# Source order on the compute engines, and mixer visits pipelined by hand, in a hybrid mLSTM/GLA encoder layer

## The chip, the cores and the metric

The kernel runs on one core of a Trainium2 chip. A core has five engines, each with an instruction stream of its own: TensorE (matrix products, PE in the profile; its weight loads are PEld), VectorE (DVE), ScalarE (ACT), GpSimd (POOL) and SyncE (SP, which here only issues DMAs). They wait for one another by semaphores. The metric is the device time of one execution in microseconds; lower is better.

## The reference

One encoder layer on a sequence of 1024 tokens with 1024 features, in float32: a token mixer, then a gated MLP, each between RMSNorms and added to the residual.

```python
def hybrid_mixer(hn, w_in, ...):
    proj = jnp.matmul(hn, w_in)
    a_qk, a_v, a_o, a_gates, b_q, b_k, b_v, b_r, b_lr = jnp.split(proj, idx, axis=-1)
    qk = silu(dwconv3(a_qk, mlstm_conv_w, mlstm_conv_b))          # q and k of 4 mLSTM heads
    i_fw, f_fw, i_bw, f_bw = jnp.split(a_gates + mlstm_gate_b, 4, axis=-1)
    h = mlstm_chunkwise(...forward...) + flip(mlstm_chunkwise(...backward...))
    y_a = sigmoid(a_o) * head_rms_norm(h, mlstm_norm)
    la = log_sigmoid(lr @ w2 + gb) / 16                           # decay per key dimension, both directions
    o = gla_chunkwise(...forward...) + flip(gla_chunkwise(...backward...))
    y_b = silu(b_r) * head_rms_norm(o, gla_norm)                  # 4 GLA heads
    return jnp.matmul(concatenate([y_a, y_b]), w_out)

x = x + rms_norm(hybrid_mixer(rms_norm(x), ...))
x = x + rms_norm(conv_ffn(rms_norm(x), ...))
```

Both scans go in both directions. Within a chunk they are products of queries and keys weighted by decays; between chunks a state is carried by "decay times state plus keys times values".

## The kernel before, in words

The sequence is cut into 8 chunks of 128 tokens. The kernel normalises and transposes the input, and computes a first strip of the projection that holds the gate columns and half of the GLA values (product `vacc`, up to about 48 us). Then two generators run interleaved:

- `proj()` computes the rest of the projection in 11 groups of 256 columns. Each matrix is split in a high and a low half, so one output takes three products. `f_block` makes 128 columns by 512 tokens (`facc`, 24 products 512 wide), `t_block` 256 tokens by 256 columns (`tacc`, 48 products 256 wide). Both `yield` three times within a block, and once more after the block's result is taken out of PSUM, so a block is four steps; each group begins with an empty step. The order is GLA keys and queries (`in_bqk`), GLA values (`in_v`, which sets `bv`), the convolved mLSTM queries and keys (`in_aqk`, `aqk`: VectorE adds the neighbours in lines 454 and 455, and after two blocks multiplies by the tanh in line 466), mLSTM values (`av`), and two gate groups (`in_gate`, `gate`). Weights of the next group are loaded and split (`wprep`, `ahead`, line 113) at the end of a group's second block.
- `mix()` is everything that needs the projection: `gla_decay` (eight products `z`, ScalarE's Abs, Exp and Ln, then VectorE lines 390, 391 and 393), `gate_rows` (row-wise gate arithmetic with four scans, lines 316 to 360), their transposes (`ptc`), then `gla()`, `mlstm()` and `out_weights()`.

In `gla()`, `levels(c)` makes a chunk's weighted scores in eight levels (64, 32, 16, 8, 4, 2, 1, 0): GpSimd takes differences `D`, ScalarE their exponential `E`, VectorE multiplies it into queries and keys (`Q`, `K`, `kz`), TensorE makes the products `sc`, and they are kept in `Pt`. `states()` makes each chunk's state (`ptk`, `U`, then `state_step` in line 537), forward as the chunks come and backward in a loop after them. `finish(c)` makes a chunk's output `o` and its head norm. `mlstm()` has `states()` (`ptm`, `KT`, `Um`, `both_step`), and for each chunk `decays` (loads and exponentials `RB`, `RI`), `front` (`sr`) and `back` (`nd`, and the division). `out_weights()` loads eight slabs of the output weights through three buffers that later hold gated rows (`yv`, `gv`), and splits them (lines 108 and 109). `prep(t)` loads and gates the rows of the output projection and transposes them (`pt`, line 888); the output product is `oacc`.

What sets the order of the work: the program is traced by `_interleave`, which gives each generator's step a weight (a projection step 0.25, a mixer step 1.0 or what it yields). From that order a planner places the instructions of each engine by its own estimates of when their inputs are ready; it decides the final order in each engine's stream and in SyncE's queue of DMAs. On the chip each stream is then executed in that order.

PSUM, where products land, has eight banks: `pe` (2: `E`, `th`, half of the mLSTM products), `ps` (3: `z`, `ptc`, `sc`, `U`, `ptk`, `o`, `sr` and others) and `mm` (3: the projection's blocks). A tile takes a bank until its last reader is done.

After the projection come the output projection (from about 440 us), and the MLP, whose products (lines 1063 and 1221) fill the rest.

Of the kernel before, what the change touches and what calls it, by code (L numbers as in the profile page):

```python
# [17 lines left out]
P = 128  # L18
# [5 lines left out]
H = 4  # L24
# [12 lines left out]
W_PROJ = 0.25  # L37
R_AUX, R_COLS, R_GLA, R_STATES, R_ML, R_OUT = 3.4, 0.6, 0.7, 0.7, 1.9, 2.0
# [4 lines left out]
def _interleave(*gens):  # L43
    live = [[g, w, 0.0] for g, w in gens]
    while live:
        e = min(live, key=lambda v: v[2])
        e[2] += e[1]
        try:
            w = next(e[0])
            if w is not None:  # L50
                e[1] = w
        except StopIteration:
            live.remove(e)
# [3 lines left out]
def tile_encoder_layer(  # L57
# [84 lines left out]
    def wprep(src, segs):  # L142
        n = sum(s[1] for s in segs)
        wh = wp.tile([P, NK, 256], F32R, name="wh")
        wl = wp.tile([P, NK, 256], F32R, name="wl")
        for g in range(4):
            raw = wp.tile([P, 2, 256], F32, name="wraw", bufs=3)
            o = 0
            for c0, w in segs:
                nc.sync.dma_start(raw[:, :, o:o + w], src[:, 2 * g:2 * g + 2, c0:c0 + w])  # L150
                o += w
            split(wh[:, 2 * g:2 * g + 2, 0:n], wl[:, 2 * g:2 * g + 2, 0:n], raw[:, :, 0:n])
        return wh, wl
# [147 lines left out]

    def gate_rows():
# [13 lines left out]
        nc.vector.tensor_scalar(out=gi, in0=gi, scalar1=gb[:, 0:1], scalar2=None, op0=ALU.add)  # L316
# [12 lines left out]
        rm = rw.tile([R, NC, P], F32, name="rm")  # L329
        nc.gpsimd.memset(rb, 0.0)  # L330
# [38 lines left out]
        yield  # L369
        for c in range(NC):  # L370
# [4 lines left out]
            yield R_COLS * W_PROJ  # L375
        yield R_AUX * W_PROJ

# [30 lines left out]
    def ahead(b=1):  # L408
        c = next(groups, None) if b == 1 else None
        if c is not None:  # L410
            ready.append(wprep(w_in, ((c, 256),)))

    ahead()

    def in_bqk(c0, dst, scale):
        wh, wl = ready.pop(0)
# [10 lines left out]
    def in_v(c0, dst, gs=(0, 1)):  # L427
        for g in gs:
            wh, wl = ready.pop(0)
# [11 lines left out]
    def in_aqk():  # L441
        for g in range(2):
            wh, wl = ready.pop(0)
# [26 lines left out]
    def in_gate(c0, off, silu):  # L470
        for g in range(2):
            wh, wl = ready.pop(0)
            yield
            for q in range(4):
# [10 lines left out]
                if q % 2:  # L485
                    nc.sync.dma_start(dG[q // 2].rearrange("(t p) n -> p t n", p=P)[:, :, off + 256 * g:off + 256 * g + 256], s)
                yield
# [11 lines left out]
    def mix():  # L499
        yield R_AUX * W_PROJ  # L500
        yield from gla_decay()
        yield from gate_rows()
        rctx.close()
        while "bq" not in done:
            yield
        gp = mctx.enter_context(tc.tile_pool(name="gp", bufs=2, reuse_waits="tile"))
        mslots = gp.tile([P, NC, H, P + 1], F32, name="mslots", bufs=1)
# [4 lines left out]

        nc.gpsimd.memset(mslots[:, 0], 0.0)
# [25 lines left out]
        def head_norm(pool, o, dst, i, c):  # L539
# [4 lines left out]
            v = pool.tile([P, H], F32, name="rs_v")  # L544
            nc.vector.tensor_scalar(out=v, in0=ss, scalar1=1.0 / DV, scalar2=EPS, op0=ALU.mult, op1=ALU.add)
            nc.gpsimd.tensor_tensor(out=hr[:, c, i, :], in0=v, in1=mhalf[:, 0:H], op=ALU.pow)
            nc.sync.dma_start(dst, o.rearrange("p h e -> p (h e)"))

        def gla():
# [23 lines left out]
            def states():  # L573
                for c in range(NC):
                    S = lp.tile([P, H, P + 1], F32, name="S")
                    nc.sync.dma_start(S, dS[c // 4][c % 4])
                    kk = load(lp, "kk", dkk[c])
                    v = v_tile(lp, dvb, c)
                    nc.scalar.activation(gam[:, c, :], S[:, :, P], AF.Exp, scale=1.0 / TEMP)
                    E = edge_decay(S, hi, lo)  # L580
                    kd = w2k("Q", 3)
                    nc.vector.tensor_tensor(out=kd, in0=E, in1=kk, op=ALU.mult)
                    yield
                    pt = ps.tile([P, H, P], F32, name="ptk", tag="ps")
                    for h in range(H):
                        nc.tensor.transpose(pt[:, h, :], kd[:, h, :], ident)
                    KT = w2k("KT", 1)
                    nc.scalar.copy(out=KT, in_=pt)
                    yield
                    U = ps.tile([P, H, P], F32, name="U", tag="ps")  # L590
                    for h in range(H):
                        nc.tensor.matmul(U[:, h, :], KT[:, h, :], v[:, h, 0:P], start=True, stop=True)
                    state_out(slots, c, [(0, H, U)])
                    if 1 <= c < NC - 1:
                        state_step(slots, lambda c, h: gam[:, c, h:h + 1], c, 0)
                    yield
                for c in range(NC - 2, 0, -1):
                    state_step(slots, lambda c, h: gam[:, c, h:h + 1], c, 1)
                    yield

            def levels(c):
# [6 lines left out]
                kk = load(lp, "kk", dkk[c])  # L608
# [6 lines left out]
                def weigh(L):  # L615
# [9 lines left out]
                    Q, K = w2k("Q", 3), None  # L625
# [689 lines left out]
```

## Time and profile before

| | |
|---|---|
| Median of 3 runs | 1189.55 us (1189.26 to 1192.82) |
| The profiled execution | 1189.67 us, span 1187.9 us |
| TensorE busy | 1151.1 us, 97% of the span |
| VectorE, ScalarE, GpSimd busy | 878.7, 591.4, 166.5 us |
| Mean granted TensorE clock | 0.989 |
| Projection and mixer | from 48.4 us to about 440 us |

How to read the lines. A group line is: line of the kernel, engine, operation, output tile <- input tiles, shapes, count, then busy time, mean nanoseconds of one, and the idle time before them with what ended it. A line by stretches is: from:to in us, the length, then for PE, PEld, DVE, ACT and POOL the busy time and (x instructions), then the granted TensorE clock, the share of DMA time and GB/s. A waits line is: who waited, for whom, us in total, times, the longest. A line of the timeline or of the chain is: start, duration, what. In the timeline, neighbours of one kind are merged (x count), and since instructions overlap, the time of several together is less than the sum of their means. Matrix products are pipelined: the time of one says little, the distance from one to the next is what it costs.

### The profile page before, as it was taken

The numbers are of one execution on the slowest core, as the hardware profiler recorded it, in microseconds if no ns is written. First come the engines' busy times: TensorE is split into PE (matmuls) and PEld (weight loads), VectorE is DVE, ScalarE is ACT, GpSimd is POOL, SyncE is SP. The second block draws the span as 40 slices with busy tenths as digits, with TensorE's granted clock in tenths as the row PEclk, the third lists the DMA queues.
The fourth block names the chain that finished last, engine by engine and source line by source line (L and its number), as shares of the span: only waits on it lengthen the run. The fifth ranks groups of instructions, "written<-read, shape, count | busy, mean of one in ns | idle before, by whom it ended". The sixth has DMA issues, their size and how long they took to land.

```text
span 1187.9 us, 21230 instructions
## 1 busy us (share of the span) xinstructions
PE 1151.1 (97%) x7896; PEld 979.7 (82%) x7896; DVE 878.7 (74%) x1604; ACT 591.4 (50%) x1271; POOL 166.5 (14%) x240
## 2 busy tenths in 40 slices
PE   8999999999999969999999999999999999999997
PEld 7989778888989968878788888888888878888885
DVE  5676669777433557667998888888888877987666
ACT  6572686878556534446543243433433245445451
POOL 1200425665054200101000000000000000000001
PEclk9999999999989989999999999999999999999999
DMA  7453675554777385542144342333224238754245
GB/s 201 149 134 102 169 223 155 152 171 127 189 197 209 117 278 186 178 141 80 36 142 142 109 132 64 113 123 108 89 81 133 98 123 299 252 178 133 81 137 190
DMA packets 134651, 175.77 MB, mean 148 GB/s; under 512 B 24964, under 2 KB 89860, under 8 KB 134548
## 3 DMA queue, kind: packets, MB, share of 16 engines
q1 hardware_dynamic: 134116, 172.58, 47.3%
q0 software_dynamic: 432, 1.84, 0.4%
q8 instruction: 62, 1.02, 0.3%
q14 instruction: 41, 0.34, 0.1%
HBM read 126.78 MB, written 47.53 MB: 147 GB/s over the span
## 4 chain that ended last, share of the span: by engine, by line
PE 73%; DVE 7%; ACT 6%; DMA 6%; issue 3%; POOL 3%; SPq 1%; DVEq 0%; POOLq 0%; ACTq 0%
PE pr L1063 35%; PE pr L1221 17%; PE facc L171 5%; PE oacc L1002 4%; PE tacc L182 4%; PE vacc L262 2%; DMA qq<-dmqq 1%; DMA yv<-dya 1%; DMA oraw<-in_w_out_dram 1%; DVE kz L637 1%; ACT sq L543 1%; DVE slots L537 1%; POOL RB L786 1%; POOL D L621 1%; POOL D L622 1%
## 5 line engine op out<-in xcount | busy, mean ns | idle before, releaser
L1063 PE MATMUL pr<-T,ah 128*128 128x512 f32 x704 | 217.2, 389 | 1.3 <-DVE G L1101 1.3
L1063 PE MATMUL pr<-B,ah 128*128 128x512 f32 x528 | 162.8, 390 | 0.0
L1063 PEld LDWEIGHTS pr<-T,ah 128*128 128x128 f32 x704 | 132.1, 188 | 29.4 <-DVE G L1101 1.8
L1063 PE MATMUL pr<-T,al 128*128 128x512 f32 x352 | 137.0, 389 | 0.0
L182 PE MATMUL tacc<-wh,xh 128*128 128x256 f32 x448 | 130.5, 291 | 0.0
L182 PE MATMUL tacc<-wl,xh 128*128 128x256 f32 x448 | 130.0, 290 | 0.0
L182 PE MATMUL tacc<-wh,xl 128*128 128x256 f32 x448 | 127.1, 284 | 0.0
L1221 PE MATMUL pr<-dwl,dah 128*128 128x512 f32 x308 | 120.0, 390 | 0.7 <-DVE dwl L113 0.7
L1221 PE MATMUL pr<-dwh,dal 128*128 128x512 f32 x308 | 120.1, 390 | 0.0
L1221 PE MATMUL pr<-dwh,dah 128*128 128x512 f32 x308 | 119.3, 390 | 0.0
L1063 PEld LDWEIGHTS pr<-B,ah 128*128 128x128 f32 x528 | 99.0, 188 | 20.4
L1063 PE MATMUL pr<-B,al 128*128 128x512 f32 x264 | 102.7, 389 | 0.0
L112 ACT CAST dah<-ar 128x512 fp32r<-128x512 f32 x77 | 47.6, 621 | 98.0 <-PE pr L1221 44.2
L182 PEld LDWEIGHTS tacc<-wh,xh 128*128 128x128 f32 x448 | 85.5, 191 | 2.7 <-issue 0.2
L182 PEld LDWEIGHTS tacc<-wl,xh 128*128 128x128 f32 x448 | 85.5, 191 | 1.4
L182 PEld LDWEIGHTS tacc<-wh,xl 128*128 128x128 f32 x448 | 85.7, 191 | 0.3
L112 ACT CAST ah<-fraw 128x512 fp32r<-128x512 f32 x64 | 39.6, 619 | 82.7 <-PE pr L1063 49.7
L113 DVE TENSOR_TENSOR dal<-ar,dah 128x512 fp32r<-128x512 f32 x77 | 53.0, 690 | 37.0 <-ACT dah L112 36.7
L1063 PEld LDWEIGHTS pr<-T,al 128*128 128x128 f32 x352 | 66.1, 188 | 13.6
L112 ACT CAST ah<-sa 128x512 fp32r<-128x512 f32 x44 | 27.4, 622 | 83.6 <-DVE sa L943 52.9
L1221 PEld LDWEIGHTS pr<-dwl,dah 128*128 128x128 f32 x308 | 57.8, 188 | 13.1 <-DVE dwl L113 1.1
L1221 PEld LDWEIGHTS pr<-dwh,dal 128*128 128x128 f32 x308 | 57.8, 188 | 12.9 <-DVE dal L113 0.9
(292 smaller groups left out, 2536.0 us busy)
## 6 DMA issues: line engine op xcount, KB each, us to landing
ar<-dA SPq DMA_DIRECT2D x77, 256.0 KB
wraw<-in_w_in_dram SPq DMA_DIRECT2D x48, 256.0 KB
fraw<-in_ffn_w_gate_dram SPq DMA_DIRECT2D x22, 512.0 KB
fraw<-in_ffn_w_up_dram SPq DMA_DIRECT2D x22, 512.0 KB
dA<-s SPq DMA_DIRECT2D x20, 512.0 KB
dA<-sx SPq DMA_DIRECT2D x10, 768.0 KB
Y<-in_ffn_w_down_dram SPq DMA_DIRECT2D x22, 256.0 KB
S<-dS SPq DMA_DIRECT2D x16, 258.0 KB
```

What stands on the lines that cost most here:

```text
L112: nc.scalar.copy(out=hi, in_=src)
L113: nc.vector.tensor_tensor(out=lo, in0=src, in1=hi.bitcast(F32), op=ALU.subtract)
L171: nc.tensor.matmul(acc, w[:, k, cs], v[:, k, hs], start=(k == 0 and n == 0), stop=(k == NK - 1 and n == 2))
L182: nc.tensor.matmul(acc[:, i, :], v[:, k, ts], w[:, k, :], start=(k == 0 and n == 0), stop=(k == NK - 1 and n == 2))
L262: nc.tensor.matmul(acc, v[:, k, ts], w[:, k, :], start=(k == 0 and n == 0), stop=(k == NK - 1 and n == 2))
L537: nc.vector.scalar_tensor_tensor(out=sl[rs, o, h, :], in0=sl[rs, c, h, :], scalar=sc(c, h)[rs], in1=sl[rs, o, h, :], op0=ALU.mult, op1=ALU ...
L543: nc.scalar.activation(sq, o[:, h, :], AF.Square, accum_out=ss[:, h:h + 1])
L621: nc.gpsimd.tensor_tensor(out=dv[:, :, :, 0, :], in0=ref, in1=xv[:, :, :, 0, :], op=ALU.subtract)
L622: nc.gpsimd.tensor_tensor(out=dv[:, :, :, 1, :], in0=xv[:, :, :, 1, :], in1=ref, op=ALU.subtract)
L1002: nc.tensor.matmul(accs[hf], v[:, j, :], w[:, k, hf * 512:(hf + 1) * 512], start=(k == 0 and n == 0), stop=(k == NK - 1 and n == 2))
L1063: nc.tensor.matmul(acc, A[i][:, k, :], B[b][j][:, k, :], start=(k == 0 and n == 0), stop=(k == 3 and n == 2))
L1221: nc.tensor.matmul(accs[i], o[v][:, ts], o[w], start=(p == 0 and n == 0), stop=(p == NP - 1 and n == 2))
```

## The change

The change has three parts.

1. The interleaved part is placed in source order on TensorE, ScalarE, VectorE and GpSimd; SyncE's queue stays with the planner. `_interleave` now has a main generator (the mixer) and a filler (the projection): the mixer yields how many projection steps are to follow.
2. The mixer's work is cut into visits with `load`, `prep` and `emit`. In `gla()`, at visit k the loads of visit k+3, the preparation of visit k+2 and the products of visit k are emitted, then the projection steps. A visit is one pair of levels of a chunk, or one chunk's state. State products come a visit after their transposes. The backward state steps are dealt over the last state visit and chunk 1's first two visits. The mLSTM states, decays and fronts are shifted against each other likewise, and the output weights are loaded three slabs ahead.
3. Smaller moves: the copy of the backward half of `U` goes from ScalarE to VectorE; gate rows are interleaved with the decays, two decays apart; the split of a weight group is dealt over projection steps (`todo`); the head norm's last two operations come a visit later; the first keys and values of the mLSTM are loaded in tiles of their own; the first gated rows may start when half of the last gate group is out (`half`).

```diff
-W_PROJ = 0.25
-R_AUX, R_COLS, R_GLA, R_STATES, R_ML, R_OUT = 3.4, 0.6, 0.7, 0.7, 1.9, 2.0
+F_HEAD, F_DECAY, F_GATES, F_COLS = 8.0, 2.0, 8.0, 1.0
+F_LEAD, F_FIRST, F_STATES, F_GLA, F_TURN = 1.5, 2.0, 1.8, 1.9, 2.0
+F_MSTATES, F_ML, F_OUT = 1.2, 4.4, 2.0
...
+def _interleave(main, filler):
+    due = 0.0
+    for n in main:
+        due += n
+        while due >= 1.0:
+            next(filler, None)
+            due -= 1.0
+    for _ in filler:
+        pass
...
     def wprep(src, c0):
...
+        todo.append(lambda: [load(g) for g in range(3)])
+        todo.append(lambda: None)
+        todo.append(lambda: None)
         for g in range(4):
+            todo.append(lambda g=g: cut(g))     # split; after g == 0 also load(3)
...
     def mix():
-        yield from gla_decay()
-        yield from gate_rows()
+        gates_ = gate_rows()
+        next(gates_)
+        yield F_HEAD
+        for n, _ in enumerate(gla_decay()):
+            if n % 2:
+                next(gates_, None)
+            yield F_DECAY
+        for _ in gates_:
+            pass
+        yield F_GATES
+        yield from gate_cols()
...
         def state_out(sl, c, parts):
...
-                    nc.scalar.copy(out=sl[64:128, c - 1, h0:h0 + n, :], in_=u[64:128])
+                    nc.vector.tensor_copy(sl[64:128, c - 1, h0:h0 + n, :], u[64:128])
...
+                def emit_(j):                    # a state visit: U of chunk j-1, transposes of chunk j
...
+                    if j == NC:
+                        back_steps(0)
...
+            def back_steps(n):
+                for c in range(NC - 2 - 2 * n, NC - 4 - 2 * n, -1):
                     state_step(slots, lambda c, h: gam[:, c, h:h + 1], c, 1)
...
+                LV = ((64, 32), (16, 8), (4, 2), (1, 0))
+                def prep(n):
+                    pairs[n] = [(L, weigh(L)) for L in LV[n]]
...
+                def emit_(n):
+                    if c > 0 and n == 0:
+                        vo[c - 1] = v_tile(lp, dvb, c - 1)
+                    if c > 0 and n == (3 if c == 1 else 1):
+                        finish(c - 1)
+                    st["emit"](n)
+                    if c == 1 and n < 2:
+                        back_steps(n + 1)
...
+            vs = pair_visits(0) + state_visits()
+            for c in range(1, NC):
+                vs += pair_visits(c)
+            for k in range(-3, len(vs)):
+                if k + 3 < len(vs):
+                    vs[k + 3].load()
+                if k >= -2 and k + 2 < len(vs):
+                    vs[k + 2].prep()
+                if k < 0:
+                    yield F_LEAD
+                    continue
+                while vs[k].gate and vs[k].gate not in done:
+                    yield 1
+                vs[k].emit()
+                yield vs[k].fill
...
             for c in range(NC):                  # mlstm
                 if c + 2 < NC:
-                    decays(c + 2)
+                    decay_load(c + 2)
+                while late:
+                    late.pop()()
+                back(c)
                 if c + 1 < NC:
                     front(c + 1)
+                if c + 2 < NC:
+                    decays(c + 2)
+                yield F_ML
...
+    def filler():
+        for _ in proj():
+            if todo:
+                todo.pop(0)()
+            yield
+
+    E = mybir.EngineType
+    with tc.manual_schedule(engines={E.PE, E.Activation, E.DVE, E.Pool}):
+        _interleave(mix(), filler())
```

More of the change, by code (lines that the diff above doesn't have):

```diff
@@ L35, with __init__ @@
 BIG = 1e30
-W_PROJ = 0.25
-R_AUX, R_COLS, R_GLA, R_STATES, R_ML, R_OUT = 3.4, 0.6, 0.7, 0.7, 1.9, 2.0
+F_HEAD, F_DECAY, F_GATES, F_COLS = 8.0, 2.0, 8.0, 1.0
+F_LEAD, F_FIRST, F_STATES, F_GLA, F_TURN = 1.5, 2.0, 1.8, 1.9, 2.0
+F_MSTATES, F_ML, F_OUT = 1.2, 4.4, 2.0
 C_AQK, C_AV, C_AO, C_AG = 0, 512, 1024, 1536
 C_BQ, C_BK, C_BV, C_BR, C_LR = 1552, 1808, 2064, 2576, 3088
[L43 to L53, printed above, removed]
+def _interleave(main, filler):
[7 more added lines that the diff above has]
+        pass
+class Visit:
+    def __init__(self, fill, emit, prep=None, load=None, gate=None):
+        self.fill, self.emit, self.gate = fill, emit, gate
+        self.prep, self.load = (f or (lambda: None) for f in (prep, load))
 @with_exitstack
@@ L329, in gate_rows @@
         rm = rw.tile([R, NC, P], F32, name="rm")
+        rows["gate"] = (gi, gf, rm)
         nc.gpsimd.memset(rb, 0.0)
@@ L368, in gate_rows, with gate_cols @@
         yield
-        yield
+    def gate_cols():
+        gi, gf, rm = rows["gate"]
         for c in range(NC):
@@ L428, in in_v @@
         for g in gs:
-            wh, wl = ready.pop(0)
+            wh, wl = group()
             yield
@@ L590, in states @@
[L590 to L597, printed above, removed]
+                    nc.scalar.activation(gam[:, j, :], S[:, :, P], AF.Exp, scale=1.0 / TEMP)
@@ new lines, in emit, with pair_visits, load_ @@
+                def emit(n):
+                    products(pairs.pop(n))
+                    if n == 3:
+                        for b in range(4):
+                            bs = slice(32 * b, 32 * b + 32)
+                            nc.scalar.copy(out=Pt[bs, :, bs], in_=acc[bs])
+                return prep, emit
+            def pair_visits(c):
+                st = {}
+                def load_():
+                    st["prep"], st["emit"] = chunk(c)
+                def emit_(n):
[6 more added lines that the diff above has]
+                        back_steps(n + 1)
+                return [Visit(F_GLA if c else F_FIRST, lambda n=n: emit_(n), lambda n=n: st["prep"](n), load_ if n == 0 else None)
+                        for n in range(4)]
@@ L859, in out_weights, with load @@
         gpost = ow["gpost"] = op.tile([P, D], F32, name="gpost")
-        for k in range(NK):
-            raw = op.tile([P, D], F32, name="oraw", tag=("yv", "yv", "gv")[k % 3], bufs=(2, 2, 1)[k % 3])
-            nc.sync.dma_start(raw, w_out[:, k, :])
-            split_scaled(woh[:, k, :], wol[:, k, :], raw, hg[:, k, :])
-            yield
+        raws = {}
+        def load(k):
+            raws[k] = op.tile([P, D], F32, name="oraw", tag=("yv", "yv", "gv")[k % 3], bufs=(2, 2, 1)[k % 3])
+            nc.sync.dma_start(raws[k], w_out[:, k, :])
+        for k in range(3):
+            load(k)
+        yield F_OUT
+        for k in range(NK):
+            split_scaled(woh[:, k, :], wol[:, k, :], raws.pop(k), hg[:, k, :])
+            if k + 3 < NK:
+                load(k + 3)
+            yield F_OUT
+        nc.sync.dma_start(gpost, rows_of(a["norm_mix_post"][0]))
+        while "half" not in done:
+            yield 1
+        first = prep(0)
+        next(first)
         while "gate" not in done:
-            yield
-        for _ in prep(0):
+            yield 1
+        for _ in first:
             pass
-        nc.sync.dma_start(gpost, rows_of(a["norm_mix_post"][0]))
     ys = {}
```

242 lines of the change are left out of this document (137 added, 105 removed).

## The prediction

> **What bounds the kernel now.** First the head of the page, then the stretches of the projection by busy time, then TensorE's waits, then the chain of waits.
>
> ```profile
> span 1187.9 us, 21230 instructions
> PE 1151.1 (97%) x7896; PEld 979.7 (82%) x7896; DVE 878.7 (74%) x1604; ACT 591.4 (50%) x1271; POOL 166.5 (14%) x240
> ...
> 48.40:331.20 282.80, 274.71 (x3529) 240.18 (x3528) 199.83 (x413) 185.33 (x431) 108.82 (x175) 1.00 0.55 155
> 331.20:341.60 10.40, 7.47 (x40) 6.59 (x40) 3.05 (x7) 5.21 (x17) 6.85 (x4) 0.67 0.97 234
> 341.60:430.80 89.20, 87.34 (x754) 83.59 (x752) 39.94 (x138) 50.08 (x165) 26.87 (x19) 1.00 0.61 186
> 430.80:447.40 16.60, 7.25 (x21) 5.50 (x21) 8.36 (x15) 5.10 (x6) 0.00 (x0) 0.59 0.83 253
> ...
> PE pt L888 <- DVE yv L882: 8.9, 2, 8.7
> PE sc L656 <- DVE kz L637: 3.8, 5, 1.2
> PE nd L807 <- DVE RB L798: 3.1, 2, 2.9
> ```
>
> TensorE (first busy column) bounds the kernel. The change reaches only the projection, from 48.4 us to the first output product at about 440. There TensorE idles 282.8 - 274.7 = 8.1, 2.9, 1.9 and 9.4 us: 22.2 in all, 8.7 of it the one wait for the first gated rows at the end. The clock column adds to that. At a mean of 0.67 over 10.4 us, 2 x 0.33 x 10.4 = 6.9 us ran at half speed, after a wait of 2.9: some 3.4 us lost. At 0.59 over 16.6 us it is 13.6 us of half speed; 8.7 of the window is the wait, and the last 7.9 us ran at half: 3.9 lost. So a better order can win 22.2 + 7.3 = 29.5 us, 2.5% of the time, and no more except from fewer switches of work.
>
> **What the new order is worth.** One projection step ("unit") is 6 products 512 wide or 12 that are 256 wide:
>
> ```profile
> 62.87 5.47 PE facc L171 x24
> ...
> 108.81 5.94 PE tacc L182 x48
> ...
> 306.49 0.36 PE L182 MATMUL tacc<-wl,xh 128*128 128x256 f32 x1
> 306.69 0.28 PE L182 MATMUL tacc<-wh,xl 128*128 128x256 f32 x1
> ...
> 59.25 0.64 PE L382 MATMUL z<-lrx,w2r 98*128 98x512 f32 x2
> ...
> 407.86 1.16 PE L811 MATMUL nd<-mslots,RI 64*128 64x129 f32 x16
> ```
>
> A unit is 5.47/4 = 1.37 or 5.94/4 = 1.49 us (1.44 in most stretches). The code gives 187 units, 11 of them empty (the start of a group of columns); the mixer asks for 172 by the end of its last mLSTM chunk, and for 20 more while the output weights are cut.
> - Waits in mid-phase: loads and preparations now lead by two visits, so the small waits for kz, RB, qq and v should go: 8.1 + 2.9 + 1.9 = 12.9 us, and the 3.4 of clock.
> - Switches: after mixer work the first projection product takes 0.20 to the next one instead of 0.12, so 0.08 per switch. From the first z to the last nd the timeline has 219 switches; the new order has about 63 visits, 126 switches: 93 x 0.08 = 7, less 2 for switches between mixer kinds now put side by side: 5.
> - The end: units run out in the middle of the eight weight cuts, so the wait at the end stays:
>
> ```profile
> 427.66 4.94 DMA oraw<-in_w_out_dram
> 432.62 1.16 ACT woh L108
> 433.80 1.30 DVE wol L109
> 435.12 3.79 DMA yv<-dya
> 439.03 0.36 DVE yv L882
> ```
>
>   After the last unit ScalarE does a tanh and the seventh cut (0.6 + 1.2), VectorE ends it (1.3), and its buffer is what the gated rows are loaded into (3.8 + 0.4): 7.9 us with hand-overs against 8.7. Gain 0.7; the half clock behind it stays.
>
> Sum of gains: 12.9 + 3.4 + 5 + 0.7 = 22 us.
>
> **What source order costs, first place: the decays.** In before the planner puts a z product wherever it can be used. Now the eight z come two units apart, gate rows go between them on VectorE, and nothing steps round a wait.
>
> ```profile
> L390 DVE SCALAR_TENSOR_TENSOR dA<-z,dD 64x512 f32<-64x512 f32 x8 | 5.5, 682 | 10.1 <-ACT dD L386 8.2 <-DMA dS<-dA 1.8
> L391 DVE SCALAR_TENSOR_TENSOR dA<-z,dD 64x512 f32<-64x512 f32 x8 | 5.6, 694 | 0.1
> L393 DVE TENSOR_TENSOR_SCAN dA<-gmask,dA 128x516 f32<-128x516 f32 x8 | 9.8, 1220 | 0.1
> L316 DVE TENSOR_SCALAR gi<-gi,gb 36x1024 f32<-36x1024 f32 x1 | 0.7, 747 | 0.0
> L323 DVE SCALAR_TENSOR_TENSOR gf<-gf,lt 36x1024 f32<-36x1024 f32 x1 | 1.2, 1193 | 0.0
> L335 DVE TENSOR_TENSOR_SCAN rb<-rmask,gf 4x1024 f32<-4x1024 f32 x2 | 4.6, 2280 | 0.1
> L336 DVE TENSOR_TENSOR_SCAN rm<-gf,gi 4x1024 f32<-4x1024 f32 x2 | 4.6, 2280 | 0.1
> ...
> 207.19 1.89 DVE L113 TENSOR_TENSOR wl<-wraw,wh 128x512 fp32r<-128x512 f32 x3
> ...
> 68.61 0.60 ACT L384 ACTIVATE dD<-z 128x512 f32<-128x512 f32 x1 [1.90 <-PE z L382]
> 69.90 0.72 ACT L386 ACTIVATE dD<-dD,one 128x512 f32<-128x512 f32 x1
> ```
>
> z0 is issued after 7 full units: 48.4 + 7 x 1.37 = 58.0. ScalarE's three steps take 2.0, so VectorE starts at 60.4. It then does, without a gap, four decays at 0.68 + 0.69 + 1.22 = 2.6 (10.4), the two bias adds (1.5), four weight cuts (x3 take 1.9: 2.5), the gate rows' 1.2 and four scans of 2.28 (10.3), and the two reads of z4 (1.4): 26.1, to 86.5. The z tiles share three PSUM buffers, so z7 needs z4 read. TensorE reaches z7 after 7 z at 0.23, 13 full units and 14 switches: 58.0 + 1.6 + 17.8 + 1.0 = 78.4. It waits 8 us, and all units stand behind it. A wait of that length is followed by about 8 us of half clock (the row of 430.8): 4 more. Bounds: 5 if the cuts run early, 10 if ScalarE adds to it. ScalarE itself stands behind the gate exponentials until about 99, but three projection banks last until about 102: no further cost. I take 12 with the clock.
>
> **Second place: states and chunk 1.** The convolution's columns (units 52 to 85) now lie under the GLA states, the backward state steps and chunks 1 and 2, all of which want VectorE.
>
> ```profile
> 157.23 1.13 DVE L537 SCALAR_TENSOR_TENSOR slots<-slots,gam 64x128 f32<-64x128 f32 x4
> 182.01 3.49 DVE L537 SCALAR_TENSOR_TENSOR slots<-slots,gam 64x128 f32<-64x128 f32 x8
> 185.72 4.39 DVE L537 SCALAR_TENSOR_TENSOR slots<-slots,gam 64x128 f32<-64x128 f32 x16
> ...
> L299 DVE COPY gst<-sacc 16x512 f32<-16x512 f32 x2 | 1.4, 697 | 1.1 <-ACT lrx L287 1.1
> L454 DVE SCALAR_TENSOR_TENSOR stg<-facc,cw,stg 128x511 f32<-128x511 f32 x8 | 6.0, 745 | 6.2 <-ACT stg L453 6.1
> L629 DVE TENSOR_TENSOR Q<-E,qq 128x512 f32<-128x512 f32 x48 | 33.0, 687 | 7.3 <-ACT E L624 6.6 <-DMA qq<-dqq 0.2
> L637 DVE TENSOR_TENSOR kz<-E,kk 64x256 f32<-64x256 f32 x80 | 33.3, 417 | 0.6
> ...
> 148.00:190.20 42.20, 40.90 (x253) 32.51 (x251) 32.19 (x80) 32.06 (x64) 14.17 (x17) 1.00 0.72 206
> ```
>
> In before 42.2 us of full TensorE work covered this stretch, with VectorE busy for 32.2 and most of chunk 1's preparation still outside. Now, from the fifth state visit to the last backward step, VectorE has (0.6 for one of 512 columns in a row of them): 5 copies to slots that were ScalarE's (3.0, priced by L299), 16 forward steps (4.6), 24 backward steps at 0.27 to 0.44 (6.5 to 10.5; 8.4), a key product (0.6), chunk 1's weighing (9.8), three convolution blocks at 1.5 (4.5), four tanh products with one wait (3.2), four cuts (2.4), a masked copy (0.2): 36.7. TensorE has 14 full units (19.1), 4 sets of products U (0.9 each) and 4 of transposes (0.45), three pair products (0.6 each) and switches (1): 27.3. The first product of chunk 0's output needs the last backward step, so about 9 us become waits, one of them near 6, with 3.5 of half clock: 12.5. Bounds 6 and 13 before the clock.
>
> The Trainium skill, page "GPSIMD Engine Reference", lists GpSimd's SBUF interfaces as shared with VectorE, with contention where a VectorE instruction has two SBUF inputs. The trace agrees: the 8 steps beside GpSimd's D took 0.44 each, the 16 without it 0.27; by that rule all 24 take the upper price, and the sum rises by 2.
>
> **Small ones.** The first GLA visit waits for memsets that begin only when the gate columns are out: 1. The first mLSTM keys wait for the released GLA memory: 0 to 4, taken as 2.
>
> Sum: 12 + 12.5 + 1 + 2 = 27.5 lost, 22 won: 5.5 slower. The profiled execution took 1189.67, 0.1 above the median of 1189.55, so 1195.
>
> The Trainium skill, page "TensorE: Matmul & The Clock Gate", Part 1, has the clock fall to half after one idle window of about 3.4 us and come back after about 3.4 us of work. By that each long wait costs 1.7 instead of 4 or 3.5, and the sum would be 1191; the rows here show half clock for 6.9 and 7.9 us after waits of 2.9 and 8.7.
>
> **The rivals.**
> - Faster: VectorE's lags stay covered. For it: VectorE is only 74% busy, and in before the same work cost TensorE almost no wait in these stretches. Against: z7 has a fixed buffer count, and 26.1 us of VectorE work stand against 20.4 of TensorE's. It decides if the lag at z7 and at chunk 0's output is under 3 us at both: 1189.7 - 22 + 3 = 1171. With one place covered: 1183.
> - Still slower: loads come late, and an engine that waits for one now holds all behind it.
>
> ```profile
> 145.06 5.77 DMA S<-dS
> ```
>
>   S takes 5.8 to land; a GLA visit is 1.9 x 1.44 + 0.8 = 3.5, and preparation starts one visit after the load: 2.3 per chunk over 7 chunks is up to 16 if no slack is left, so up to 1211; I take 1205. Against: the products come two visits later still.
> - The change doesn't do what it says: SyncE's queue isn't under the order, so loads stand where the planner puts them, not three visits ahead. That gives the case above, or, where they stand earlier, none of it.
>
> **How the numbers follow.** Both waits as worked out: 45%, 1195 (1190 to 1201). One covered: 22%, 1183. Neither: 13%, 1171. Late loads besides: 20%, 1205. The range of 8 in 10 goes from 1172 to 1208. A measurement of this kernel tells about 0.3%, 3.6 us, from no change: faster is the third case and most of the second (0.31), the same the rest of the second and the lower end of the first (0.17), slower the others (0.52).
>
> **What would show it.** In the changed profile: a TensorE wait at z near 78 us of about 8 for VectorE L391, with the clock at half behind it; waits for kz and for slots between 160 and 215; the row of kz waits at 3.8 gone; the wait for the first gated rows still 7 to 9. The forecast is wrong if z waits under 3 us, or if TensorE waits often for DMA.

## The result, and the profile after

| | before | after |
|---|---|---|
| Median, runs side by side (4 each) | 1190.59 us | 1234.29 us (1233.64 to 1236.68) |
| Ratio, 95% interval | | 1.0369 (1.0346 to 1.0392) |
| First output product begins | 441.4 us | 487.7 us |

The change makes the kernel 44 us slower; 5.5 were forecast, and the range ended at 1208. The page's head of the changed kernel, with TensorE:

```profile
span 1231.9 us, 21201 instructions
PE 1151.0 (93%) x7896; PEld 984.6 (80%) x7896; DVE 905.0 (73%) x1611; ACT 589.6 (48%) x1264; POOL 167.3 (14%) x240
```

TensorE's busy time is what it was (1151.1); the span has grown by 44.0. The stretches of the projection show where:

```profile
77.00:90.00 13.00, 4.03 (x11) 3.16 (x11) 12.76 (x10) 1.10 (x2) 0.35 (x4) 0.61 0.27 68
90.00:107.20 17.20, 15.52 (x72) 11.98 (x70) 13.35 (x22) 10.16 (x17) 0.62 (x6) 1.00 0.24 60
107.20:120.70 13.50, 7.82 (x36) 6.60 (x36) 2.10 (x4) 2.80 (x10) 2.85 (x6) 0.62 0.59 156
120.70:186.00 65.30, 61.58 (x666) 54.78 (x665) 43.38 (x86) 40.64 (x82) 26.40 (x37) 1.00 0.74 211
186.00:206.00 20.00, 9.79 (x149) 7.64 (x149) 19.50 (x47) 7.82 (x17) 7.14 (x11) 0.74 0.21 54
206.00:300.00 94.00, 76.74 (x1472) 67.95 (x1471) 69.08 (x147) 60.17 (x160) 47.35 (x71) 0.96 0.46 128
356.00:380.00 24.00, 15.31 (x101) 14.35 (x101) 13.17 (x25) 10.52 (x27) 7.69 (x4) 0.79 0.76 197
478.60:489.30 10.70, 3.69 (x11) 2.56 (x12) 6.14 (x12) 3.84 (x5) 0.00 (x0) 0.68 0.91 265
```

Length less the first busy column is TensorE's idle time: 9.0, 1.7, 5.7, 3.7, 10.2, 17.3, 8.7 and 7.0 us. What TensorE waited for, from the rows of its waits:

```profile
PE sc L728 <- ACT acc L740: 9.8, 4, 6.0
PE facc L186 <- DVE wl L118: 9.0, 1, 9.0
PE pt L1021 <- DVE yv L1015: 7.0, 1, 7.0
PE ptc L394 <- ACT cols L395: 5.7, 1, 5.7
PE ptm L848 <- DMA mkk<-dmk: 5.3, 1, 5.3
PE sc L726 <- DVE acc L743: 5.1, 3, 2.2
PE nd L926 <- DVE RB L917: 3.3, 1, 3.3
PE sc L728 <- ACT ob L803: 3.3, 2, 2.3
```

The same stretch of GLA visits in the kernel before idles 3.8:

```profile
206.00:300.00 94.00, 90.21 (x1967) 82.45 (x1966) 70.38 (x160) 74.48 (x210) 58.62 (x89) 1.00 0.50 147
```

From 48.4 us to the first output product the time divides into three: TensorE idle, what half clock costs (half of the time in which TensorE was busy at a granted clock of 0.5), and the rest.

| us | before | after | change |
|---|---|---|---|
| TensorE idle | 22.2 | 64.1 | +41.9 |
| lost to half clock | 4.0 | 17.7 | +13.7 |
| rest: products and switches | 366.7 | 357.5 | -9.2 |

Together 46 longer; from the first output product on the changed kernel is 2.3 shorter. So the new order does save TensorE 9.2 us, and the waits that come with it cost six times that. In the two timelines TensorE changes between projection and mixer products 219 times before and 142 times after; if the changes are all of the 9.2, they cost 0.12 us each, which no run isolates. Two of the rows are short stories in the timeline. First VectorE in the head, and between 186 and 206 us:

```profile
76.26 2.28 DVE L354 TENSOR_TENSOR_SCAN rb<-rmask,gf 4x1024 f32<-4x1024 f32 x1
78.47 2.25 DVE L355 TENSOR_TENSOR_SCAN rm<-gf,gi 4x1024 f32<-4x1024 f32 x1
80.74 2.28 DVE L354 TENSOR_TENSOR_SCAN rb<-rmask,gf 4x1024 f32<-4x1024 f32 x1
82.95 2.25 DVE L355 TENSOR_TENSOR_SCAN rm<-gf,gi 4x1024 f32<-4x1024 f32 x1
85.23 0.69 DVE L118 TENSOR_TENSOR wl<-wraw,wh 128x512 fp32r<-128x512 f32 x1
...
188.98 3.02 DVE L573 SCALAR_TENSOR_TENSOR slots<-slots,gam 64x128 f32<-64x128 f32 x8
...
194.46 0.84 DVE L709 TENSOR_TENSOR kz<-E,kk 64x256 f32<-64x256 f32 x2
...
196.72 2.23 DVE L573 SCALAR_TENSOR_TENSOR slots<-slots,gam 64x128 f32<-64x128 f32 x8
```

Then ScalarE (in brackets: idle before, and what ended it):

```profile
112.10 0.62 ACT L117 CAST wh<-wraw 128x512 fp32r<-128x512 f32 x1 [5.88 <-DMA wraw<-in_w_in_dram]
112.62 0.55 ACT L395 COPY cols<-ptc 128x108 f32<-128x108 f32 x3
...
195.40 0.60 ACT L495 ACTIVATE th<-stg 128x512 f32<-128x512 f32 x1 [4.61 <-DVE kz L709]
...
199.76 0.60 ACT L696 ACTIVATE E<-D 128x512 f32<-128x512 f32 x1 [2.27 <-DVE stg L496]
...
201.60 0.27 ACT L740 COPY acc<-sc 128x128 f32<-128x128 f32 x1
```

The wait of 9.0 near 77 is a weight cut that is ready (ScalarE's part of it ended at 73.8) but stands behind four scans. The wait of 5.7 at 107 is four copies of gate columns that free PSUM, behind a weight cast whose DMA has not landed. The wait of 6.0 that ends at 201.9 is the copy at 201.60. ScalarE comes to it late twice over: a tanh stands 4.6 us for a PSUM bank that VectorE gives back with the kz of 194.46, behind eight backward steps, and then an exponential (199.76) stands 2.3 us for VectorE's line 496, behind the next eight. Each time something ready stands behind something that waits.

### The profile page after: what moved, and what is told of

Same layout as the page of the kernel before. It is cut to its first block, busy times and chain, and to the rows that moved or that the text cites. A ratio compares the mean times of both kernels' runs of the same rounds, so it can differ in the third digit from the quotient of the medians.

```text
span 1231.9 us, 21201 instructions
## 1 busy us (share of the span) xinstructions
PE 1151.0 (93%) x7896; PEld 984.6 (80%) x7896; DVE 905.0 (73%) x1611; ACT 589.6 (48%) x1264; POOL 167.3 (14%) x240
## 4 chain that ended last, share of the span: by engine, by line
PE 71%; DVE 13%; ACT 5%; DMA 4%; issue 4%; POOL 2%; SPq 0%; DVEq 0%; POOLq 0%; ACTq 0%
PE pr L1204 32%; PE pr L1362 16%; PE tacc L197 8%; PE oacc L1143 6%; PE vacc L277 2%; PE facc L186 2%; DVE kz L709 1%; DVE Q L701 1%; PE nd L926 1%; DVE wl L118 1%; DMA wraw<-in_w_in_dram 1%; ACT E L696 1%; DVE T L118 1%; PE nd L930 1%; DMA dS<-dA 1%
## 5 line engine op out<-in xcount | busy, mean ns | idle before, releaser
L197 PEld LDWEIGHTS tacc<-wh,xh 128*128 128x128 f32 x448 | 87.3, 195 | 2.7
L1204 PEld LDWEIGHTS pr<-T,al 128*128 128x128 f32 x352 | 66.1, 188 | 13.7
L1362 PEld LDWEIGHTS pr<-dwh,dah 128*128 128x128 f32 x308 | 57.8, 188 | 13.0 <-ACT dah L117 1.1
```

The lines of the kernel that those rows point to most:

```text
L197: nc.tensor.matmul(acc[:, i, :], v[:, k, ts], w[:, k, :], start=(k == 0 and n == 0), stop=(k == NK - 1 and n == 2))
L1204: nc.tensor.matmul(acc, A[i][:, k, :], B[b][j][:, k, :], start=(k == 0 and n == 0), stop=(k == 3 and n == 2))
L1362: nc.tensor.matmul(accs[i], o[v][:, ts], o[w], start=(p == 0 and n == 0), stop=(p == NP - 1 and n == 2))
```

## The experiments

Each ratio below is to the kernel before in runs on the same chip, with its 95% interval. "Changed kernel" is the kernel after. Differences in us between two versions are taken from medians of different chips; the intervals are 2 to 6 us to either side, so 3 or 4 us between two versions can't be told from none. "Idle and half clock" adds TensorE's idle time and what half clock costs, as in the table above.

**Is it the order?** The changed kernel with the planner placing all engines, and the text of before in source order:

```diff
# e1_planner: the changed kernel
-    with tc.manual_schedule(engines={E.PE, E.Activation, E.DVE, E.Pool}):
-        _interleave(mix(), filler())
+    _interleave(mix(), filler())
# e2_order_alone: the kernel before
-    _interleave((proj(), W_PROJ), (mix(), 1.0))
+    with tc.manual_schedule(engines={E.PE, E.Activation, E.DVE, E.Pool}):
+        _interleave((proj(), W_PROJ), (mix(), 1.0))
```

> The changed program without the line that keeps source order: the planner places all engines again, from the new program order. Theory A (waits come from the order: an engine that stands before one operation holds all behind it) expects the new waits of 67 us in the projection to fall to 30 or less and 1180 to 1200 us. Theory B (the new program order itself is bad: convolution under the VectorE-heavy chunks, mixer early) expects 1220 to 1235.

> The kernel before, with source order on the four engines and nothing else. Theory A expects waits at each dependence, since nothing is pipelined in its source: 1300 us or more. Theory B expects little change, under 1210, since its program order is the one that was good.

Measured: e1 1200.97 us, 1.0100 (1.0061 to 1.0138); e2 1325.94, 1.1155 (1.1104 to 1.1206). Source order costs the new text some 33 us, and it would have cost the old text 138: the hand pipelining does what it is for, but does not make up for the planner. What remains in e1, about 12 us, is the new text under the planner. One of its waits stands in the head, and one of 4.1 for ScalarE (line 1149) behind the projection, at the start of the MLP; e8, e10, e13 and e16 have that one too, neither the kernel before nor the changed kernel does. The row is the one in the head:

```profile
PE z L403 <- DVE dA L412: 5.7, 1, 5.7
```

**Two single causes, guessed wrong.** More projection steps between the decays, and each visit's products ahead of the preparation two visits on:

```diff
# e3_head_fill
-F_HEAD, F_DECAY, F_GATES, F_COLS = 8.0, 2.0, 8.0, 1.0
+F_HEAD, F_DECAY, F_GATES, F_COLS = 8.0, 3.0, 8.0, 1.0
# e4_products_first: in gla()'s loop
-                if k >= -2 and k + 2 < len(vs):
-                    vs[k + 2].prep()
...
                 vs[k].emit()
+                if k + 2 < len(vs):
+                    vs[k + 2].prep()
```

> The changed kernel with three projection steps after each decay in place of two: 8 steps (11 us) move from the end to the head. If VectorE's 26 us of decays, gate scans and weight cuts against 20 us of TensorE work make the wait of 9.0 at 77 us, it falls under 2 with its 4 us of half clock, the wait at the end grows from 7 to about 14, and the time is 1225 to 1230. If the wait only moves to the next place where VectorE is needed (the gate columns), the time stays at 1234 or rises to 1242.

> The changed kernel with the products of visit k, and the copies that empty their PSUM banks, emitted ahead of the preparation of visit k+2. If the 27 us of waits between 186 and 292 come from bank-freeing copies that stand behind preparations on ScalarE and VectorE, they fall under 10 and the half clock there from 10 to 3: 1205 to 1216 us. If they come from VectorE's load alone, the preparations get later and the time stays within 1228 to 1240.

Measured: e3 1237.97, 1.0414 (1.0366 to 1.0461); e4 1231.32, 1.035 (1.0312 to 1.0389). In e3 the wait of 9.0 is gone and four others stand between 87 and 112 us (3.2, 4.7, 2.3 and 1.7, one for a z and three for weight cuts). In e4 the waits for bank-freeing copies shrink and waits for kz, a prepared operand, grow from 1.2 to 10.2. The GLA stretch idles less, but at half clock:

```profile
206.00:300.00 94.00, 80.25 (x1527) 71.71 (x1529) 68.76 (x147) 62.29 (x163) 46.65 (x72) 0.91 0.45 129
```

Idle and half clock together are 20.8 us there, against 20.3 in the changed kernel: nothing is gained. Idle time alone misleads in such a stretch. In e17 below, whose edit only touches the mLSTM, the stretch idles 12.6 instead of 17.3, but loses 8.4 to half clock instead of 3.0. Moving one thing past another only chose who waits.

**One standing copy, and which engine.** In the GLA visits ScalarE's longest idle time is not for the preparation:

```profile
ACT Pt L767 <- DVE acc L743: 18.7, 5, 5.5
ACT E L696 <- POOL D L694: 8.7, 13, 1.3
```

These rows are ScalarE's waits from 206 to 300 us in the changed kernel. At a chunk's last visit the copy of the diagonal blocks into Pt waits for VectorE, which keeps the last level behind the next preparation; all exponentials stand behind that copy. e5 issues it a visit later. e6, e7 and e8 take ScalarE, VectorE, or all but TensorE out of the source order:

```diff
# e5_diag_later
                     products(pairs.pop(n))
+                    while diags:
+                        diags.pop()()
                     if n == 3:
-                        for b in range(4):
-                            bs = slice(32 * b, 32 * b + 32)
-                            nc.scalar.copy(out=Pt[bs, :, bs], in_=acc[bs])
+                        diags.append(diag)       # the same four copies
# e6_act_free / e7_dve_free / e8_pe_order_only
-    with tc.manual_schedule(engines={E.PE, E.Activation, E.DVE, E.Pool}):
+    with tc.manual_schedule(engines={E.PE, E.DVE, E.Pool}):          # e6
+    with tc.manual_schedule(engines={E.PE, E.Activation, E.Pool}):   # e7
+    with tc.manual_schedule(engines={E.PE}):                         # e8
```

> The changed kernel, with one thing moved: the four copies of the diagonal blocks into Pt (line 767) are issued after the next visit's products instead of right behind their own. In the changed kernel ScalarE stands there 23.8 us in all (8 times) until VectorE has kept the last level. Theory A (that standing wait holds the exponentials E and the bank-freeing copies behind it): TensorE's waits for sc between 206 and 300 us, about 27 us together, fall by half or more: 1215 to 1222 us. Rival (the round from GpSimd's D over E to Q is itself longer than a visit's work on TensorE, so the wait goes elsewhere): 1230 to 1236.

> The changed kernel, with ScalarE taken out of the source order (the planner places its stream; TensorE, VectorE and GpSimd keep source order). TensorE waits 24.6 us in all for ScalarE in the changed kernel (acc 9.8, cols 5.7, ob 3.3, stg 1.7, KT 1.6, Pt 1.9, sq 0.6). Theory A1 (ScalarE's order is the larger part): 1206 to 1215. Rival A2 (each of the two engines holds the other, so with one freed the wait moves to VectorE, whose waits are 26): 1220 to 1234.

> The changed kernel, with VectorE taken out of the source order (TensorE, ScalarE and GpSimd keep it). TensorE waits 26.4 us for VectorE before the end of the phase (weight cut 9.0, acc 8.2, RB 3.3, slots 2.9, K 1.8, kz 1.2) and 7.0 at the end. If VectorE's order is the larger part: 1202 to 1212, and the 9.0 for the weight cut near 77 us gone. If the two hold each other: 1220 to 1234.

> The changed kernel, with TensorE alone in source order and the other engines placed by the planner. If the hand-written order of TensorE is sound and the loss comes from the engines that feed it: about the 1201 of the version with all engines placed by the planner, or below it (1190 to 1203). If TensorE's own order is the loss (products placed where their inputs are not ready): 1218 to 1234.

Measured: e5 1226.82, 1.0302 (1.0255 to 1.035); e6 1235.18, 1.0366 (1.0308 to 1.0424); e7 1224.29, 1.0289 (1.0242 to 1.0335); e8 1212.38, 1.0189 (1.0137 to 1.024). In e5 the copy's wait is out of ScalarE's rows, and the stretch from 206 to 300 idles 10.1 us instead of 17.3:

```profile
206.00:300.00 94.00, 83.89 (x1654) 74.58 (x1653) 72.30 (x154) 66.08 (x175) 52.68 (x79) 0.96 0.47 134
```

Idle and half clock there fall from 20.3 to 12.8. So theory A holds with 7.5 us there and 7.5 in the time, less than it said; its 27 had counted waits from 186 on, and this stretch idles 17.3. e6 fell short altogether: up to 300 us its trace saves 5.4 of idle and half clock (the head alone 7.5), and loses that behind, where a wait of 4.1 at 411.9 with no cause in the profile and 4.5 us more after the first output product stand. In the GLA stretch part of the waits went over to VectorE, first row of TensorE's waits in e6, against 5.1 in the changed kernel; e7 gains 10 us, and its GLA stretch falls from 20.3 to 10.3 of idle and half clock; in its head (second fence) a z takes the cut's place with the same 9.1:

```profile
PE sc L726 <- DVE acc L743: 9.3, 3, 5.2
PE facc L186 <- DVE wl L118: 9.1, 1, 9.1
```

```profile
PE sc L728 <- ACT acc L740: 9.4, 4, 6.0
PE z L403 <- DVE dA L412: 9.1, 1, 9.1
```

A sum of waits by engine is therefore no price for that engine's order. Freed together (e8) the feeders give back 22 us, and TensorE's own order accounts for the other 11 between e8 and e1. In e8 the GLA stretch is clean: TensorE's order there is the hand-written one, VectorE has the same work, and it idles 3.4 us at full clock, where the kernel before idles 3.8. But 77 to 90 and 186 to 206 still idle 8.2 and 7.6.

```profile
206.00:300.00 94.00, 90.63 (x1888) 83.09 (x1889) 76.58 (x166) 71.53 (x192) 58.06 (x83) 1.00 0.51 148
```

**The head, and the backward steps.** e9 deals the scans out one by one between decays and cuts weights one block earlier; e10 is e1 with the gate rows behind the decays; e11 leaves the backward state steps out.

```diff
# e9_head_spread: a yield after each scan, early cuts, and
-            if n % 2:
+            if n in (1, 3, 4, 5, 6):
                 next(gates_, None)
-        c = next(groups, None) if b == 1 else None
+        c = next(groups, None) if b == 0 else None
# e10_planner_decays_first: e1, and
-            if n % 2:
-                next(gates_, None)
# e11_no_back_steps
             def back_steps(n):
+                return
```

> The changed kernel (all four engines in source order) with the head dealt otherwise: the four scans over gate rows (2.28 us each on VectorE) are issued one by one between decays 3 to 6 instead of all four in a row, and the weights of the next column group are loaded and cut one block earlier. The projection steps that the mixer asks for are the same. Theory H (the row of scans stands ahead of the weight cut and of the later decays on VectorE: waits of 9.0, 1.7 and 5.7 us with half clock behind two of them): the wait for the weight cut near 77 goes, and at least half of the 16 us with it: 1212 to 1222. Rival (VectorE has more work up to 112 us than the projection steps given there cover, so the wait moves to a z or to the gate columns): 1228 to 1238.

> The version in which the planner places all engines from the new program order (1201 us), with the gate rows traced behind all eight decays, as in the kernel before, instead of between them. Its trace has one wait of 5.7 at a z product, for the read of an earlier z that stands behind four scans on VectorE, and 6.8 us of half clock after it. If these are what the new program order costs: 1190 to 1195. If the other waits (nd 5.8 for ScalarE and 3.3 for VectorE, 4.1 after the projection) are it, and this one moves: 1198 to 1203.

> The changed kernel without the 24 backward state steps (VectorE line 573 for the backward half, 8.8 us in three rows of 8 between 189 and 206 us); the backward states are then not carried from chunk to chunk. In the changed kernel TensorE idles 10 us of 186 to 206 and runs at half clock for about 10 more. If VectorE's amount of work there is the cause (the term that the forecast put at 12.5): 1220 to 1226, with the idle of that stretch down to 3 or less. If only the order in which the tanh, the exponentials and the bank-freeing copies stand is: 1231 to 1236.

Measured: e9 1228.94, 1.0303 (1.0265 to 1.0341); e10 1202.83, 1.0093 (1.0064 to 1.0123); e11 1224.42, 1.0277 (1.0248 to 1.0306). In e9 and in e10 the waits moved to the gate columns, as the rivals had it. The rows are e9's and e10's:

```profile
PE ptc L395 <- DVE gf L380: 5.1, 1, 5.1
...
PE ptc L395 <- DVE gi L373: 2.8, 1, 2.8
```

```profile
PE ptc L394 <- DVE gi L372: 5.8, 1, 5.8
```

Up to 120 us idle and half clock fall from 21.9 to 15.4 in e9, and rise from 8.2 (e1) to 14.2 in e10. VectorE idles less than 5 of the 40 us from 61 to 101 in all of these, so the next guess is that TensorE needs more projection steps in that time. In e11 the stretch from 186 to 206 idles 3.7 us instead of 10.2, with half clock 6.9 instead of 13.9, and the time falls by 10: the backward steps are the cause there. Whether by their amount or by their place ahead of other work e11 doesn't tell, since it takes away both. In e1 VectorE does the same 24 steps between 175 and 191 us, and TensorE idles 2.6 from 186 to 206; in e8, where only TensorE is held to its order, it idles 7.6.

```profile
186.00:206.00 20.00, 16.27 (x260) 13.01 (x260) 18.39 (x39) 12.08 (x31) 9.42 (x15) 0.83 0.38 99
```

**More steps in the head.** e12 is e9 with ten more steps there and e5's copies; e13 is e10 with six more; e14 is e13 with steps moved from GLA to mLSTM visits.

```diff
# e12_source_more_fill
+F_HEAD, F_DECAY, F_GATES, F_COLS = 8.0, 2.5, 14.0, 1.0
# e13_planner_more_fill
+F_HEAD, F_DECAY, F_GATES, F_COLS = 8.0, 2.0, 14.0, 1.0
# e14_planner_refilled: e13, and
-F_LEAD, F_FIRST, F_STATES, F_GLA, F_TURN = 1.5, 2.0, 1.8, 1.9, 2.0
-F_MSTATES, F_ML, F_OUT = 1.2, 4.4, 2.0
+F_LEAD, F_FIRST, F_STATES, F_GLA, F_TURN = 1.5, 2.0, 1.8, 1.65, 2.0
+F_MSTATES, F_ML, F_OUT = 1.2, 4.9, 2.0
```

> Source order on four engines, the scans dealt out and the weight cuts early (1229 us), and two more things: ten more projection steps in the head (F_DECAY 2.5, F_GATES 14), and the diagonal copies a visit later (worth 7.5 us by their own run). Theory F (VectorE's work in the head is more than the steps given there cover): the head's four waits (11.3 us together) and the half clock behind them go: 1203 to 1212. Rival (the wait moves once more, or the ten steps are missed at the end of the phase): 1218 to 1226.

> The planner's version with the gate rows traced behind the decays (1203 us), and six more projection steps before the gate columns (F_GATES 14 for 8). Theory F: the wait of 5.8 us at the gate columns and the 17 us of half clock behind it (8.5 lost) go: 1188 to 1194. Rival (the wait goes elsewhere, or the steps are missed at the end): 1198 to 1204.

> The same as the planner's version with six more steps in the head, and besides fewer projection steps per GLA visit (1.65 for 1.9) and more per mLSTM chunk (4.9 for 4.4), where TensorE waited 9.7 us in all for the readers of nd. If those waits are a lack of projection steps there: 3 to 5 us below the version with six more steps, 1184 to 1190. If they come from the order of the readers, or the GLA visits then wait for VectorE: the same as it or up to 6 slower.

Measured: e12 1220.45, 1.0233 (1.0186 to 1.028); e13 1194.42, 1.0023 (1.0004 to 1.0043); e14 1198.13, 1.0076 (1.0045 to 1.0107). In e13 the wait at the gate columns is gone and the time is 8 lower, though a wait of 7.4 now stands at the next group's weight cut. So the gain did not come from the head, where idle and half clock up to 120 us are 15.0 against 14.2 in e10; later waits shrank (idle to the first output product 31.5 in e10, 22.0 in e13). In source order the ten steps did help the head (9.4 in e12, 15.4 in e9). In e12 the steps are missed at the end, where the wait for the first gated rows doubles:

```profile
PE pt L1029 <- DVE yv L1023: 14.5, 3, 13.8
```

e14 found no gain in the mLSTM and lost at the end (7.2 for yv against 4.0).

**The last places.** e15 is e13 with the earlier cuts of e9; e16 is e15 with the gate rows traced in six pieces; e17 is the changed kernel with the mLSTM's first decay loads two and three visits earlier.

```diff
# e15_planner_early_cuts: e13, and
-        c = next(groups, None) if b == 1 else None
+        c = next(groups, None) if b == 0 else None
# e16_planner_rows_dealt: e15, a yield after each scan, and
         for _ in gates_:
-            pass
-        yield F_GATES
+            yield 2.3
+        yield F_GATES - 12
# e17_decay_loads_first
-                    if n in (2, 4):
-                        decay_load(n // 2 - 1)
+                    if n in (0, 1):
+                        decay_load(n)
```

> The planner's version with six more projection steps in the head (1194 us), and the weights of the next column group loaded and cut one block (four steps) earlier. In that version TensorE waits 7.4 us at 94.7 for a cut that stands behind the decays and gate rows on VectorE, with 20.5 us of half clock behind it (10 lost). If the cut's place is the cause: 1177 to 1183, 0.7 to 1.1% below the kernel before. If VectorE's amount of work there is, the wait moves to the gate columns or to a z: 1190 to 1196.

> The planner's version with six more projection steps and early cuts (1187 us), with the gate rows traced in six pieces, one per 2.3 projection steps, instead of in one piece behind the decays (the number of steps up to the gate columns grows by two). If the wait of 7.4 us for the cut comes from its standing behind the gate rows: it goes, with most of the 20.5 us at half clock: 1170 to 1177. If VectorE's amount of work up to there is the cause, the wait moves to the gate columns or a later cut: 1184 to 1190.

> The changed kernel, with the loads for the first two mLSTM chunks' decays issued in the first and second state visit of the mLSTM instead of the third and fifth. If the keys are late because these seven transfers stand ahead of theirs (mkk issued at 354.52, landed at 361.6): the wait of 5.3 and most of the 3.3 for RB go, with the half clock behind them: 1222 to 1228. If the transfers now stand ahead of the first keys instead, or the two key buffers set the pace: 1231 to 1238.

Measured: e15 1186.74, 0.9979 (0.9963 to 0.9995); e16 1201.73, 1.0092 (1.0062 to 1.0121); e17 1238.29, 1.0398 (1.036 to 1.0436). e15 is the best version, 0.2% below the kernel before, which is under the 0.3% that the prediction took as what a measurement tells. It hit neither expectation: its wait in the head is where it was (first two rows). The GLA stretch idles 2.5 us (third row) where e13's idled 5.0, at full clock instead of 0.96, but that is lost again before the first output product, which begins at 442.8 (441.5 in e13). The gain stands behind the projection: e13's wait of 4.1 there is gone, and the part after the first output product is 7.1 us shorter. That the early cut does this is not shown.

```profile
94.50:102.00 7.50, 0.12 (x2) 0.05 (x1) 7.39 (x15) 2.92 (x5) 0.00 (x0) 0.64 0.35 91
102.00:117.00 15.00, 15.00 (x74) 13.82 (x75) 2.99 (x5) 3.96 (x12) 3.13 (x7) 0.50 0.36 97
...
206.00:300.00 94.00, 91.48 (x1945) 84.37 (x1944) 79.14 (x173) 73.08 (x198) 57.17 (x85) 1.00 0.55 162
```

In e16 the head did get better: 4.4 us of wait and little half clock, instead of 7.4 and 15 us busy at half, 8.9 us in all.

```profile
101.00:105.40 4.40, 0.04 (x1) 0.04 (x1) 4.16 (x6) 3.23 (x6) 0.00 (x0) 1.00 0.05 7
105.40:109.00 3.60, 3.60 (x20) 3.31 (x20) 1.80 (x3) 2.94 (x7) 0.00 (x0) 0.53 0.50 116
```

But from 120 us to the first output product its waits and half clock cost 33.0 us against e15's 17.2, and the part after it 7 more. Why an edit of the head moves the planner's choices 100 to 400 us later stays open. e17 shows SyncE's queue. In the changed kernel the keys (mkk) are issued behind seven transfers and a weight load, 5 us after the transposes at 348.93 had freed their buffer:

```profile
349.37 0.62 SPq L894 DMA_DIRECT2D kko<-dmk  x1
350.03 0.59 SPq L898 DMA_DIRECT2D RB<-drr  x1
...
352.27 1.23 SPq L559 DMA_DIRECT2D qq<-dmqq  x2
...
354.52 0.44 SPq L599 DMA_DIRECT2D mkk<-dmk  x1
```

With these loads earlier the keys behind them are late earlier: the long wait for mkk is now at 342.8, for the keys issued at 339.10 behind kko, RB, RI and qq; their buffer was free only at 337.4, so the two key buffers set part of that pace. The row is e17's, and the wait is not saved, but spread; e17's time doesn't differ from the changed kernel's beyond the noise:

```profile
PE ptm L848 <- DMA mkk<-dmk: 4.8, 2, 3.6
```

## Why the prediction was wrong

Right were the sign, the places that it named and, at one of them, the size; which products would wait there it had wrong. For each term the forecast, and what it measured (idle plus half clock):

| step | forecast | measured |
|---|---|---|
| waits in mid-phase | -16.3 | 206 to 300 us alone: 17.3 + 3.0, where before has 3.8 idle |
| switches | -5 | -9.2 (all of the "rest"), with 142 switches for the forecast's 126 |
| the end | -0.7 | wait 7.0 for 8.7 |
| the head | +12 | 9.0 + 1.7 + 5.7, and 5.9 of half clock: 22.3 |
| states and chunk 1 | +12.5 | 186 to 206: 10.2 + 3.7 = 13.9 |
| first GLA visit | +1 | 1.8 |
| mLSTM start | +2 | 8.7 + 4.1 = 12.8 |

**The step that failed** is the first gain: "loads and preparations now lead by two visits, so the small waits for kz, RB, qq and v should go". The small waits for kz did go (3.8 to 1.2), but waits for the copies that free PSUM came in their place, so that the term of -16.3 became 20.3 lost in the GLA visits alone. Of the 38 us that the forecast fell short, some 20 are this step, 10 the head and 11 the mLSTM's start, and the switches gave back 4. The preparations do lead, but in the same streams as those copies, so a copy waits for whatever the lead put ahead of it, and turned round (e4) the preparations wait for the copies. What the forecast weighed was late loads and VectorE's amount of work. A standing copy on ScalarE that holds the exponentials (18.7 us there) was not among it. e5 took 7.5 us off the kernel by moving that one copy, and e7, with VectorE's stream free, 10. e8 shows that the order of the feeding engines is the whole of it there: with them free and TensorE's order kept, the stretch loses 3.4.

**The head.** The place, VectorE's walk and the length of the wait were right: four scans from 76.3 to 85.2 and z4's reads behind them, which it had ending at 86.5 and which end at 87.3. The victim was another: no z waited, which the forecast had named as a sign of being wrong, but the next group's weight cut, which stands in the same stream. That the size still came out is partly luck; in e7, with VectorE free to put the cut first, it was a z. What the step left out is ScalarE's copies of the gate columns at 107. The forecast said that the banks "last until about 102: no further cost". They lasted until 100.2 (the wait of 1.7), and at 107 a cast that waited for its DMA held the copies that free others.

**States and chunk 1.** Right in size and in the work that causes it: e11, with VectorE's backward steps out, loses 6.9 there. The victim was another here too: chunk 0's output (`o`) begins at 207.0 without a wait, and the 2.9, 1.2 and 6.0 us stand at `sc`. The 1.8 of the first GLA visit is not the memsets either: TensorE waits for line 704, behind a product that waited 2.3 us for its load of `qq`.

**mLSTM start.** Taken as 2 for released memory; it was the queue of SyncE, which the third rival had named in general, by the issue times above. e17 moved that wait but did not remove it, so what the queue alone costs stays open.

**Half clock.** The forecast took 3.5 to 4 us behind each long wait. The rows:

```profile
86.00:89.90 3.90, 3.90 (x9) 3.12 (x10) 3.74 (x5) 0.00 (x0) 0.00 (x0) 0.50 0.32 87
...
112.90:120.60 7.70, 7.68 (x34) 6.50 (x35) 0.54 (x1) 2.00 (x8) 2.75 (x6) 0.50 0.39 97
```

After the wait of 9.0 the clock was half for 3.9 us of work, 2.0 lost; after that of 5.7 for 7.7, 3.8 lost. The rule of the Trainium skill, page "TensorE: Matmul & The Clock Gate", Part 1, that some 3.4 us of work bring the clock back, fits the first and not the second, nor e15's 15 us. The forecast erred more by the number of waits than by their price: seven of 2.9 us or more, where it had three (8 in the head, near 6 at the states, and the end).

## What to carry to other kernels

Source order on several engines at once is a promise that no ready instruction stands behind a waiting one; before making it, follow for every engine what the lead puts ahead of the copies that free PSUM. A wait that the profile books to one engine is not what freeing that engine gains: of 24.6 us e6 gained 5.4 up to 300 us and nothing in the time. Compare stretches by idle time and half clock together, since one stands in for the other. And where an engine runs almost without a gap (VectorE, 61 to 101 us), dealing its work out moved the wait on (e9, e10); more other work for TensorE helped there in source order (e12), and was missed at the end.

## What the runs showed of the hardware that was not expected

The time that the clock stays at half after a wait varies widely: 3.9 us of work after 9.0 of wait, 7.7 after 5.7 (the rows above), and in e15 15 us of uninterrupted work after 7.4. There the 256-wide products are 0.21 us apart at first, where at full clock it is 0.12 (e15's timeline; 0.12 in the changed kernel at 350 us). In e16, after 4.4 us of wait at nearly the same place, it was about 3.4.

The kept traces show what goes with the long spells. By the granted clock, every spell at half between 48 and 490 us lasts a whole multiple of 3.41 us (79.7 to 90.0 and 110.4 to 120.7 in the changed kernel: three each). Of such stretches that TensorE worked through without a gap, 15 did not bring the clock back; 14 of them hold 3 to 12 of the 36x36 transposes `ptc` among the wide products. Of the 148 stretches that did bring it back, six hold any (1 to 6). Whether the transposes are the cause no run tried.
